# Two fused transformer blocks on one core: the instruction order derived with the other machine model

## The chip, the cores and the metric

The kernel runs on one core of a Trainium2 chip. Its engines are TensorE (PE, with its weight load shown apart as PEld), VectorE (DVE), ScalarE (ACT), GpSimd (POOL) and SyncE (SP, which here issues transfers). The metric is the device time in microseconds. Three runs of the kernel before took 1939.66, 1941.54 and 1941.79 us, median 1941.54 us.

## The reference

The input is one sequence of 512 tokens of width 1024, all in float32. It goes through two blocks of one layer each.

```
first_block:
  proj = rmsnorm(x) @ w_in            # 9792 columns: z, xbc, dt, q, k, v, gates
  y_ssd  = ssd_branch(...)            # conv + silu, 32 heads, two directions, chunks of 128 tokens
  y_attn = window_attention(q, k, v, ...) @ w_attn_out
  x = x + rmsnorm((g_ssd * y_ssd + g_attn * y_attn) @ w_o)
  x = x + rmsnorm(square(relu(rmsnorm(x) @ w_mlp_in)) @ w_mlp_out)
second_block:
  x = x + parallel_mixer(rmsnorm(x))  # mLSTM heads and latent causal attention, then one product
  x = x + memory_cross_attention(rmsnorm(x), rmsnorm(mem))
  x = x + square(relu(rmsnorm(x) @ w_ff1)) @ w_ff2
```

## The kernel before

**Products.** All large products use float32r, whose operands are split in two parts (`hi + lo`). Each product takes three matmuls per tile of 128 rows: hi by hi, lo by hi and hi by lo (lines 266 to 268 where channels are the output's partitions, `cm`; lines 284 to 286 where tokens are, `tm`). A full `cm` step is 24 matmuls of 512 columns into one PSUM bank `psg`, of which there are two; in the SSD stage it is cut into two half steps of 12. A `tm` step is 24 matmuls of 256 columns.

**Weights.** They come as a stream of units of 1 MB. SP loads a unit into one of two `raw` buffers (line 129), ACT casts it to `whi` in two halves (line 140) and DVE subtracts to get `wlo` (line 141). `use()` asks for the split of the next unit while the present one is multiplied.

**Stages.** First norm and the decays (about 0 to 50 us). The SSD branch in eight groups of four heads (to about 520 us, with a plain output product at 300 to 350 us). Window attention in eight pairs of heads with the gates between them (to 850 us). A residual norm (850 to 910), the first feed-forward (to 1240), the mixer and the attention to the memory (to 1600), the second feed-forward (to the end).

**What sets the order.** The body is traced as one straight list of instructions, the source order. In the SSD stage each group's steps and the next group's products (`f0` to `f7`) are listed by hand, and so are those of the mixer (`SEQ`) and of the attention to the memory (`XSEQ`):

```
GSEQ = """
z0 w0 xt1 st0 z1 w1 z2 z3 st1 silu st2 y0 f0 f1 y1 rows f2 f3 w2 e0 y2 e1 w3 f4 f5 bt cb y3 norm f6 e2 f7 u0 u1 xt0 e3
"""
```

The source order isn't the order that the engines get. When the `TileContext` is left, the framework plays the list through a model of the machine. In it an instruction can be issued when its inputs are ready in the model's time and its buffer is free, and where several can, the one that is earlier in the source goes first. The order in which the model issued them is then fixed for each engine. On the chip each engine runs its own list in that order and stops at an instruction whose semaphore has not come, with everything behind it. A few places bind the order by hand: `tc.issue_after` (lines 165, 182, 443, 559) and `tc.keep_in_program_order` (line 394).

**Lines that the prediction speaks of.** `late` and `dt_evac` with the round trip of the decays through DRAM (`csd`, `gld`, lines 500 and 513, fetched on POOL's queue at 626 and 628); the exponents (663 to 670); the convolution with its silu (567 to 573); `to_tokens` (578, 579); `cb` (634); `weights` (675); `y` (683 to 702); `norm` (707) and `u_channels` (712, which ends in `split_from`, 317 and 318).

Of the kernel before, what the change touches and what calls it, by code (L numbers as in the profile page):

```python
# [43 lines left out]
# columns of w_in  # L44
Z0, XBC0, DT0, Q0, K0, V0, G0 = 0, 2048, 6144, 6208, 7232, 7488, 7744
# columns of w_in_2
U0, VM0, OP0, IF0 = 0, 512, 1024, 1536

# columns of the packed constants
# [3 lines left out]
def packed_constants():  # L53
    """Constants that depend on shapes alone: the identity and its mirror image, the rotary
    frequencies, the one-hot of the relative position buckets, and the fixed rows of the products
    that make the exponents of the decays."""
# [11 lines left out]
    # rows 0..7 choose the chunk, rows 64..127 the pair that a token is in  # L68
# [4 lines left out]
    # rows 8..15 choose the head, rows 64..127 hide the pairs of tokens that a direction doesn't see  # L73
# [11 lines left out]
def body(ctx, tc, a, out, dbg=None):  # L85
# [26 lines left out]
    # ---------------------------------------------------------------- weights, as a stream of blocks  # L112
    win, win2 = a["w_in"][0], a["w_in_2"][0]

    class Unit:
        """A block of weights [128, kt, n], split into two parts of float32r whose sum it is."""
# [36 lines left out]
    def use(key, lag=False):  # L153
        """The unit; the next one is split at once or, with lag, where ahead() says."""
        stream[pos[key]].split()
        if not lag:
            ahead(key)
        return unit_of[key]

    def ahead(key, *behind):  # L160
        """The next unit being split, behind the given instructions, and the one after it on its way."""
        i = pos[key]
        with ExitStack() as order:
            for ins in behind:
                order.enter_context(tc.issue_after(ins.ins))
            for u in stream[i + 1 : i + 2]:
                u.split()
        for u in stream[i + 2 : i + 3]:
            u.load()

    def evac_first(key, evac, *args):
        """evac, with the next unit's split behind the first of it on each engine."""
# [78 lines left out]
    # ---------------------------------------------------------------- helpers  # L251
    def cm(key, act, evac, parts=1):
        """Steps of a channel-major product: evac(j, psum) for each 128 columns of the unit, each in
        one step or more."""
# [19 lines left out]
    def tm(key, act, evac, ntile=NT):  # L274
        """Steps of a token-major product: evac(t, psum) for each 128 tokens."""
# [20 lines left out]
    def weave(main, side):  # L296
        """The steps of both lists, each list spread evenly."""
# [13 lines left out]
    def split_from(src, hi, lo, gain=None):  # L311
        """hi + lo = src * gain (a column of gains), both float32r."""
# [7 lines left out]
    def inv_rms(dst, ssq, n, width):  # L320
        """dst = (ssq / n + eps) ** -0.5 for [128, width] columns."""
# [3 lines left out]
    def token_sums(ssq, tag="t"):  # L325
        """Sums over the partitions of [128, 512], token-major in PSUM [128, 4]."""
# [5 lines left out]
    def bcast_tokens(r, tag="t"):  # L332
        """[128, 4] token-major -> PSUM [128, 512] on every partition."""
# [5 lines left out]
    # ---------------------------------------------------------------- persistent tiles  # L339
# [17 lines left out]
    # ---------------------------------------------------------------- block 1, first norm  # L357
# [12 lines left out]
    # the tensor engine's clock is at its full rate when the first inputs are here  # L370
# [34 lines left out]
    # ---------------------------------------------------------------- parameters, as columns  # L405
# [34 lines left out]
    # ---------------------------------------------------------------- dt and the decays  # L440
# [14 lines left out]
    # what the products for the exponents take: see ssd_exponents  # L455
# [4 lines left out]
    def dt_evac(_, po):  # L460
        """Rows (half, direction, head), two chunks of tokens in each half."""
# [17 lines left out]
        # cumulative sums of dt * a in each chunk, forwards and backwards  # L479
# [13 lines left out]
        # cs in two float32r parts, by way of DRAM, where the heads of a group are one row  # L493
# [8 lines left out]
        # the logarithm of dt, less cs, in two parts too  # L502
# [11 lines left out]
        # token-major: exp(cs) and dt * exp(tot - cs)  # L514
# [14 lines left out]
        def late():  # L529
# [8 lines left out]
            # the decay over a whole chunk, on every partition; step k takes chunk k and chunk 3 - k  # L538
# [25 lines left out]
    # ---------------------------------------------------------------- block 1, SSD branch  # L564
# [22 lines left out]
    class Group:  # L587
        """The SSD branch of one group of four heads."""
# [5 lines left out]
        # products, convolution and layouts  # L594
# [27 lines left out]
        # rows of the products for the exponents  # L622
# [32 lines left out]
        def exponents(self, c):  # L655
            """dt[s] exp(cs[l] - cs[s]) of both directions: cs[l] comes from rows 0..7,
            log(dt) - cs[s] from rows 8..15; rows 64..127 hide what overflows on the wrong side, and
            the select what is next to the diagonal."""
# [110 lines left out]
    # ---------------------------------------------------------------- block 1, window attention  # L769
# [8 lines left out]
    # the bias over relative positions, one row for each head, read back as a Hankel block: the  # L778
    # queries of each block are taken in reverse
# [18 lines left out]
    def keys(kv):  # L798
        """The two parts of the keys of a head, each on both halves of the partitions."""
# [11 lines left out]
    def q_steps(u, parts=1):  # L811
        """Queries of a head, in reverse in each block: one part on its own half of the partitions,
        the other part on the other half."""
# [935 lines left out]
```

## Time and profile before

| what | value |
|---|---|
| three runs, median | 1941.54 us |
| profiled execution, first to last instruction (its span) | 1939.5 us |
| what the profile gives of its time outside the span | nothing; the three runs lie 0.2 to 2.3 us above the span |
| PE busy | 1868.0 us, 96% |
| weight load (PEld) busy | 1541.4 us, 79% |
| DVE, ACT, POOL busy | 1083.4 us (56%), 856.8 us (44%), 482.8 us (25%) |
| mean granted TensorE clock | 0.992 of full speed |

Read it from PE down: PE has a record open in 96% of the span, so 71.5 us of the span have none. A matmul's record is longer than the distance to the next one, so the distance between starts, not the length of a record, tells the rate. The other engines' shares say little by themselves: they are averages over stages, and in the SSD stage DVE is busy three quarters of the time, in the feed-forwards a third.

### The profile page before, as it was taken

The page shows a single profiled execution, that of the slowest core. Times are in us where ns is not written, and L with a number is a line of the kernel's source. Part 1 is how long each engine was busy: PE and PEld are TensorE (multiplying, and loading weights), DVE is VectorE, ACT ScalarE, POOL GpSimd, SP SyncE. Part 2 cuts the span into 40 slices and gives each one's busy share as a digit, 9 for nine tenths or more (in the row PEclk, how much of TensorE's full clock was granted, in tenths as well). Part 3 has the DMA queues.
Part 4 walks back from the last instruction along what each step waited for, and adds up shares of the span by engine and source line. Part 5 has one row for each costly group of instructions (what it writes and reads, how often), then busy time and mean ns, then how long its engine had stood idle before and what let it go on. Part 6 is the DMA issues. An engine that isn't in the chain of part 4 may idle for free. (4 is left out here: it accounts for less than half of the span.)

```text
span 1939.5 us, 24660 instructions
## 1 busy us (share of the span) xinstructions
PE 1868.0 (96%) x9685; PEld 1541.4 (79%) x9685; DVE 1083.4 (56%) x1751; ACT 856.8 (44%) x1397; POOL 482.8 (25%) x530
## 2 busy tenths in 40 slices
PE   8989999999999999998999999989999999999999
PEld 6878778887887777887888888888877778888887
DVE  7767773777555654537334334667567763334543
ACT  5655652755335665345332323444453543323231
POOL 1544450444202221233011202322110431111020
PEclk9999999999999999999999999999999999999999
DMA  6222122221222221333333332322111213232322
GB/s 174 68 67 67 45 67 87 67 67 44 82 94 82 82 78 66 119 122 109 98 109 98 101 94 89 114 73 74 51 45 65 87 44 108 90 107 87 109 87 65
DMA packets 169377, 164.10 MB, mean 85 GB/s; under 512 B 8742, under 2 KB 165101, under 8 KB 169262
## 3 DMA queue, kind: packets, MB, share of 16 engines
q1 hardware_dynamic: 157322, 151.03, 24.8%
q10 hardware_dynamic: 9444, 9.89, 1.6%
q0 software_dynamic: 2496, 1.61, 0.3%
q8 instruction: 76, 1.25, 0.3%
q14 instruction: 39, 0.32, 0.1%
HBM read 158.26 MB, written 4.23 MB: 84 GB/s over the span
## 5 line engine op out<-in xcount | busy, mean ns | idle before, releaser
L141 DVE TENSOR_TENSOR wlo<-raw,whi 128x1024 fp32r<-128x1024 f32 (+2 forms) x285 | 374.9, 1329 | 277.8 <-ACT whi L140 275.4
L140 ACT CAST whi<-raw 128x1024 fp32r<-128x1024 f32 (+2 forms) x285 | 288.3, 1029 | 408.9 <-PE psg L267 381.1
L266 PE MATMUL psg<-hh,whi 128*128 128x512 f32 (+1 forms) x1016 | 403.0, 397 | 0.8 <-DVE hl L318 0.8
L267 PE MATMUL psg<-hl,whi 128*128 128x512 f32 (+1 forms) x1016 | 400.7, 394 | 0.0
L268 PE MATMUL psg<-hh,wlo 128*128 128x512 f32 (+1 forms) x1016 | 399.3, 393 | 0.0
L266 PE MATMUL psg<-ua_h,whi 128*128 128x512 f32 x800 | 316.5, 396 | 0.5 <-DVE xT L1562 0.5
L267 PE MATMUL psg<-ua_l,whi 128*128 128x512 f32 x800 | 313.4, 392 | 0.0
L268 PE MATMUL psg<-ua_h,wlo 128*128 128x512 f32 x800 | 312.3, 390 | 0.0
L266 PEld LDWEIGHTS psg<-hh,whi 128*128 128x128 f32 (+1 forms) x1016 | 191.0, 188 | 40.5 <-issue 1.2
L268 PEld LDWEIGHTS psg<-hh,wlo 128*128 128x128 f32 (+1 forms) x1016 | 190.7, 188 | 39.7
L267 PEld LDWEIGHTS psg<-hl,whi 128*128 128x128 f32 (+1 forms) x1016 | 190.8, 188 | 38.1 <-DVE hl L315 0.4
L1164 POOL TENSOR_TENSOR fsq<-relu 128x512 f32<-128x512 f32 x64 | 80.9, 1264 | 507.9 <-ACT relu L1161 434.5
L266 PEld LDWEIGHTS psg<-ua_h,whi 128*128 128x128 f32 x800 | 150.1, 188 | 35.4 <-DVE xT L1562 2.4
L267 PEld LDWEIGHTS psg<-ua_l,whi 128*128 128x128 f32 x800 | 150.3, 188 | 32.3 <-DVE ua_l L1165 1.2
L268 PEld LDWEIGHTS psg<-ua_h,wlo 128*128 128x128 f32 x800 | 150.2, 188 | 30.7
L284 PE MATMUL psg<-whi,hh 128*128 128x256 f32 x416 | 121.5, 292 | 2.7 <-ACT sz L608 2.7
L286 PE MATMUL psg<-whi,hl 128*128 128x256 f32 x416 | 121.8, 293 | 0.0
L285 PE MATMUL psg<-wlo,hh 128*128 128x256 f32 x416 | 120.5, 290 | 1.0 <-DVE wlo L141 1.0
L986 POOL TENSOR_TENSOR ssq<-ssq,sq 128x512 f32<-128x512 f32 x42 | 66.4, 1582 | 117.0 <-ACT sq L985 116.0
L1165 DVE TENSOR_TENSOR ua_l<-fsq,ua_h 128x512 fp32r<-128x512 f32 x64 | 47.3, 739 | 79.2 <-POOL fsq L1164 79.2
L284 PEld LDWEIGHTS psg<-whi,hh 128*128 128x128 f32 x416 | 81.5, 196 | 5.9 <-ACT sz L608 4.0
L285 PEld LDWEIGHTS psg<-wlo,hh 128*128 128x128 f32 x416 | 81.4, 196 | 1.6 <-DVE wlo L141 1.2
(560 smaller groups left out, 2910.4 us busy)
## 6 DMA issues: line engine op xcount, KB each, us to landing
raw<-in_w_in_dram SPq DMA_DIRECT2D x37, 1024.0 KB
raw<-in_w_ff_dram SPq DMA_DIRECT2D x32, 1024.0 KB
raw<-in_w_mlp_in_dram SPq DMA_DIRECT2D x16, 1024.0 KB
raw<-in_w_mlp_out_dram SPq DMA_DIRECT2D x16, 1024.0 KB
raw<-in_w_in_dram SPq DMA_DIRECT2D x16, 512.0 KB
raw<-in_w_ssd_out_dram SPq DMA_DIRECT2D x8, 1024.0 KB
raw<-in_w_attn_out_dram SPq DMA_DIRECT2D x4, 1024.0 KB
raw<-in_w_o_dram SPq DMA_DIRECT2D x4, 1024.0 KB
```

Source lines behind the costliest of these rows:

```text
L140: A.copy(self.hi[sl], self.raw[sl])
L141: V.tensor_tensor(out=self.lo[sl], in0=self.raw[sl], in1=self.hi[sl].bitcast(F32), op=ALU.subtract)
L266: T.matmul(o, lhsT=u.hi[:, k, c:e], rhs=xh[k], start=k == 0, stop=False)
L267: T.matmul(o, lhsT=u.hi[:, k, c:e], rhs=xl[k], start=False, stop=False)
L268: T.matmul(o, lhsT=u.lo[:, k, c:e], rhs=xh[k], start=False, stop=k == u.kt - 1)
L284: T.matmul(o, lhsT=xh[k][:, tk], rhs=u.hi[:, k, 0 : u.n], start=k == 0, stop=False)
L285: T.matmul(o, lhsT=xh[k][:, tk], rhs=u.lo[:, k, 0 : u.n], start=False, stop=False)
L286: T.matmul(o, lhsT=xl[k][:, tk], rhs=u.hi[:, k, 0 : u.n], start=False, stop=k == u.kt - 1)
L986: G.tensor_tensor(out=self.t, in0=self.t, in1=q, op=ALU.add)
L1164: G.tensor_tensor(out=f, in0=r, in1=r, op=ALU.mult)
L1165: V.tensor_tensor(out=ua_l[:, m, :], in0=f, in1=ua_h[:, m, :].bitcast(F32), op=ALU.subtract)
```

## The change

One argument is added where the kernel opens the framework's context. The machine model that the scheduler plays the source order through is another one, which follows each engine's queue of issued instructions and the semaphores between the engines, and has its own durations. The source order, the instructions, the buffers and the hand-made bindings stay. The rest of the diff replaces comments and docstrings by blank lines, so that line numbers stay too.

```diff
-    with tile.TileContext(nc) as tc:
+    with tile.TileContext(nc, schedule_with_timeline_sim=True) as tc:
         body(tc, aps, out)
```

## Rows read from the trace of the kernel before

**Rows 1.** The page: each engine's busy time, share of the span and instructions
```profile
PE 1868.0 (96%) x9685; PEld 1541.4 (79%) x9685; DVE 1083.4 (56%) x1751; ACT 856.8 (44%) x1397; POOL 482.8 (25%) x530
```

**Rows 2.** Busy time by stage: length, PE, PEld, DVE, ACT, POOL, clock, DMA share, GB/s
```profile
0.00:40.00 40.00, 37.57 (x194) 30.44 (x195) 28.96 (x66) 22.80 (x39) 6.21 (x21) 1.00 0.60 174
40.00:300.00 260.00, 234.06 (x1330) 199.81 (x1329) 196.52 (x286) 150.79 (x231) 121.49 (x173) 0.96 0.23 67
350.00:520.00 170.00, 159.13 (x915) 134.44 (x914) 126.83 (x191) 95.93 (x149) 69.62 (x97) 0.99 0.20 61
520.00:850.00 330.00, 328.57 (x1796) 265.02 (x1796) 168.11 (x358) 162.00 (x305) 73.11 (x53) 1.00 0.30 96
850.00:910.00 60.00, 54.95 (x289) 44.21 (x288) 41.09 (x48) 31.22 (x51) 22.66 (x15) 1.00 0.24 72
910.00:1240.00 330.00, 330.00 (x1472) 273.10 (x1471) 125.99 (x137) 105.92 (x142) 52.12 (x44) 1.00 0.32 102
1240.00:1600.00 360.00, 338.91 (x1977) 276.09 (x1976) 248.05 (x510) 169.21 (x321) 89.08 (x89) 1.00 0.21 66
1890.00:1939.50 49.50, 44.81 (x212) 36.57 (x210) 17.97 (x25) 8.29 (x13) 0.22 (x1) 0.98 0.21 64
```

**Rows 3.** PE's waits, whole span: waiting line, releaser, us in total, times, longest
```profile
PE psc L634 <- ACT cT L573: 8.6, 6, 2.3
PE pse L663 <- DMA lh<-gld: 6.9, 1, 6.9
PE pst L712 <- DVE ua_l L318: 5.8, 4, 2.6
...
PE pst L712 <- DVE sz L707: 4.7, 5, 1.3
PE pst L578 <- DVE ua_l L318: 4.7, 4, 1.6
```

**Rows 4.** PE in order of time, SSD: start, length, line, tiles, count [idle before]
```profile
215.63 0.39 PE L266 MATMUL psg<-hh,whi 128*128 128x512 f32 x1
...
218.12 0.39 PE L268 MATMUL psg<-hh,wlo 128*128 128x512 f32 x1
218.35 0.94 PE L712 MATMUL pst<-ident,sz 128*128 128x128 f32 x4
...
227.71 0.28 PE L285 MATMUL psg<-wlo,hh 128*128 128x256 f32 x1
229.57 0.66 PE L578 MATMUL pst<-ident,cacc 128*128 128x128 f32 x4 [1.58 <-DVE ua_l L318]
229.99 0.36 PE L286 MATMUL psg<-whi,hl 128*128 128x256 f32 x1
```

**Rows 5.** All engines in order of time: the first exponents, columns as in rows 4
```profile
49.99 1.19 PE L663 MATMUL pse<-rh,lh 128*128 128x512 f32 x2 [6.93 <-DMA lh<-gld]
```

**Rows 6.** One of six stretches with a lowered granted clock, columns as in rows 2
```profile
44.00:56.00 12.00, 6.01 (x35) 5.76 (x36) 9.49 (x15) 6.01 (x9) 1.41 (x6) 0.72 0.64 184
```

**Rows 7.** ACT by line: count, busy us, mean ns, idle before and releasers
```profile
L140 ACT CAST whi<-raw 128x1024 fp32r<-128x1024 f32 (+2 forms) x285 | 288.3, 1029 | 408.9 <-PE psg L267 381.1 <-issue 11.4 <-PE pse L1226 9.6
L1162 ACT ACTIVATE ua_h<-relu 128x512 fp32r<-128x512 f32 x64 | 40.4, 631 | 0.9
...
L665 ACT ACT_TABLE_LOAD x25 | 32.1, 1283 | 0.4
L573 ACT ACT_TABLE_LOAD x23 | 29.5, 1283 | 0.4
```

**Rows 8.** ACT in order of time: a table load between two functions, columns as in rows 4
```profile
55.05 1.28 ACT L665 ACT_TABLE_LOAD   x1
56.35 0.60 ACT L665 ACTIVATE e<-pse 128x512 f32<-128x512 f32 x1
```

**Rows 9.** DVE by line, columns as in rows 7
```profile
L141 DVE TENSOR_TENSOR wlo<-raw,whi 128x1024 fp32r<-128x1024 f32 (+2 forms) x285 | 374.9, 1329 | 277.8 <-ACT whi L140 275.4 <-PE psc L1296 2.2
```

**Rows 10.** The load queue's own longest wait, columns as in rows 3
```profile
SPq L129 <- DVE wlo L141: 1463.4, 121, 39.2
```

## The prediction

> **What bounds the kernel now.** I read the stage table first, then PE's waits, then PE in order of time in one SSD group. PE is the bound: a record is open for 1868.0 of 1939.5 us [rows 1]. The reader is to see in the stage table that the 71.5 us without one lie in few places [rows 2]. In the feed-forward (910 to 1240) PE is open for 330.00 of 330 us. The idle time of the others, as length less PE: start 2.4, SSD to 300 us 25.9, SSD from 350 us 10.9, attention 1.4, the residual norm 5.1, mixer and memory 21.1, the end 4.7. The sum is 71.5. So the order can change about 58 us of idle time, 36.8 in the SSD stage and 21.1 in the mixer, and it can add more.
>
> What ends the waits is a chain through other engines: silu to the products of the group (8.6 us), a fetched row of decays (6.9), evacuated PSUM banks (5.8 and 4.7) [rows 3]. DVE is busy for 196.5 of 260 us in the SSD stage, ACT for 150.8 [rows 2], so a chain step there finds another one in front of it most of the time.
>
> The clock has a part of its own. From 40 to 300 us the mean granted clock is 0.96 [rows 2], because PE runs at 1.2 instead of 2.4 GHz in stretches that follow idle time, such as 0.72 over 12 us with PE open for half of them [rows 6]. The deficit is 0.04 x 260 + 0.01 x 170 = 12.1 us of full rate, and PE has work in nine tenths of it: 10.9 us. Over 36.8 us of idle time that is 0.3 us lost again for each idle us. I multiply added or removed idle time in this stage by 1.3.
>
> **The change, part by part.** It removes and adds no arithmetic and no transfer. It moves instructions within each engine's list. Since every engine stops at its first instruction that isn't ready, a move costs when it puts a step that isn't ready in front of work that is, or puts the chain's step behind work that could have waited. Both are in the trace. At 227.71 us four transposes (L578) stand inside a run of products and hold it for 1.58 us although the next matmul of it (L286) is ready [rows 4]. The other way round, four transposes (L712) come behind a half step of 12 matmuls from 215.63 to 218.12 us: 2.49 us for 11 distances, 0.226 each, so 2.72 us for a half step [rows 4].
>
> *Feed-forwards, 910 to 1240 and 1600 to 1890: nothing.* A step of 24 matmuls lasts 24 x 0.226 = 5.4 us. Beside it ACT has an evacuation, a square (0.63 each by the square's row) and half of a unit's cast (1.03): 2.3 us [rows 7]; DVE has a split (1.33) and one more operation [rows 9]. With the two accumulator banks, an evacuation placed behind both casts is 2.1 us late and still early. If that cover were gone it would cost the 2.1 us once for each step; I take 0, bounds 0 and +2. The load queue waits 1463 us in all for buffers that `wlo` frees, on average 12 us [rows 10], so it has nothing to be reordered for; a split that comes later by one step moves the load behind it by as much, and PE has a whole unit of 10.9 us before it needs that.
>
> *Start: -2 us, bounds -7 and +5.* PE stands for 6.93 us at the first exponents [rows 5], which wait for the decays' way through DRAM. The transfer's time stays. A model with other transfer times may put ready work before them: at most the whole 6.93 us is filled. If the chain on DVE falls behind one unit's split (two of 1.33) and on ACT behind its cast (two of 1.03), it is 4.7 us longer. It is nearer to the first, since the stall shows that the old model took the rows as landed; but the ready work in the source is small, so a third.
>
> *SSD groups: +12.4 us, bounds -20 and +25.* What is to move is the interleaving of the next group's products with this group's chain. In a model that follows queues, matmuls that are ready are taken into PE's queue, and a transpose that gets ready a little later finds them in front. The unit of that delay is the half step, 2.72 us. Nothing is lost while PE works off such a step; it is lost at the group's end, where the chain then ends later and the products are used up. There are seven transitions between groups, and each already has PE waiting for the chain (nine waits at L712 alone if the second releaser of 4.7 us is counted in), so slack there is nil. Bounds: a full half step each, 7 x 2.72 x 1.3 = 24.8; or the waits at L712 and L578 (5.8 + 4.7 + 4.7) all go, -15.2 x 1.3 = -19.8. I take half a half step, 7 x 1.36 x 1.3 = 12.4, as those nine waits last 1.2 us on average.
>
> *Attention 520 to 850: 0, bounds -1.4 and +5.* PE is open for 328.6 of 330 us; ACT and DVE are busy half of the time [rows 2] and cover a moved step; the upper bound is two half steps. *Residual norm: 0, bounds -1 and +3*: one chain, whose order its data give.
>
> *Mixer and memory: +7 us, bounds -12 and +21.* 21.1 us of idle time in 360 [rows 2], DVE at 69%. The source order is a long hand-made list of short steps of four heads, as sensitive as the SSD list; I take the same share of its idle time, 12.4 / 36.8 = a third. Lower bound: over half of it goes; upper: it doubles.
>
> *Table loads: 0 in the forecast.* The order on ACT decides how often exponential and silu alternate. Now 25 loads stand before exponentials and 23 before silus, 1.283 us each, with 0.4 us of idle time before each of the two groups in all [rows 7]. They are followed without a gap too: a load begins at 55.05 and its exponential at 56.35 [rows 8], so a switch takes 1.30 us.
>
> The Trainium skill (ScalarE: Activation LUTs, section What ACT_TABLE_LOAD costs) counts a drain of about 1.38 us on top, 2.66 us for each switch. This trace doesn't agree: 1.30 us from start to start. By the page every switch that the new order adds would cost twice as much as in the rival on table loads below.
>
> Sum: -2 + 12.4 + 7 = +17.4 us on the span of 1939.5 us, 1956.9. The median of the runs lies 2.0 us above the span, so I predict 1959 us.
>
> **The rivals.**
>
> *The other order fits the chip better (faster).* One mechanism: steps that the old model held for ready too early, and that now stop PE in front of ready work, are put later. For it: the 1.58 us hold at 229.57 [rows 4], the 6.93 us at 49.99 [rows 5], and clock stretches that follow such holds. Against it: most of the waits end with a busy DVE, which another order does not make faster. Price: 4 us of the first wait and a third of the 15.2 us at L712 and L578, 9 x 1.3 = 12; in the mixer 3 of 21.1. That gives 1939.5 - 15 + 2 = 1927 us, from 1914 to 1937. It decides when the removed holds outweigh the delayed chains, which cost 1.36 us for each transition.
>
> *Nothing that counts moves (same).* The two accumulator banks, the two weight buffers and the data dependences leave each engine little choice, so that only steps with slack change places. For it: the feed-forwards, where no wait is left. Against it: in rows 4 steps of both kinds are within one another, so the list there hangs on readiness to a fraction of a us. Time: 1938 to 1945 us.
>
> *ACT's order falls apart (much slower).* The SSD stage has 40 silus and 32 pairs of exponentials. If each silu got its own load, and each exponential run between them, there would be 80 loads in place of the 48 now: 32 x 1.283 = 41 us on ACT, whose share in the stage goes from 57% (150.8 + 95.9 of 430 us [rows 2]) to 67%. The largest of PE's waits that ends with ACT is 8.6 of 71.5 us [rows 3], an eighth, so 41 / 8 x 1.3 = 7 us come through. With a mixer at its upper bound, 14 above what I took, this is 1941.5 + 17.4 + 7 + 14 = 1980 us. Against it: nothing in the change is about tables.
>
> **How the numbers follow.** Forecast (slower by 4 to 35 us) 0.44; better fit 0.31; same 0.13; much slower 0.12. A difference under 0.2%, 3.9 us, can't be told from none. So faster 0.31, within 0.2% 0.13, slower 0.56. The forecast's own range is 1946 to 1976 us (its upper end all half steps at full price). The range of 1920 to 1992 us leaves out the lower third of the better fit and the upper half of the worst case, together 0.16; it is wide because both signs have weight.
>
> **What would show it.** The stage table of the new profile: idle time between 40 and 520 us up from 36.8 to about 46 us, in the mixer from 21 to 28, none in the feed-forwards. PE's waits: more at L712, L578 and L634, less at L663. The lists: the same counts but for table loads. Granted clock in the SSD stage below 0.96. I am wrong if idle time in the SSD stage falls, if a feed-forward shows waits (then the evacuations' order was not covered), or if the time went into a stage where I put 0.

## The result, and the profile after

The changed kernel takes 2022.6 us (median of four runs, 2021.4 to 2024.2), the kernel before in the same session 1941.5 us: 1.0419 times as long, 95% interval [1.0404, 1.0434], or 81 us more. The direction is the one forecast, the size is almost five times the forecast's 17.4 us, and the time lies beyond the upper end of the range.

The page's line of the engines, to be read against [rows 1]:

```profile
PE 1906.0 (94%) x9685; PEld 1581.4 (78%) x9685; DVE 1068.5 (53%) x1751; ACT 842.1 (42%) x1384; POOL 480.6 (24%) x530
```

The counts are the same but for 13 fewer on ACT. The span has grown from 1939.5 to 2019.7 us; PE's time without a record from 71.5 to 113.7 us (2019.7 less 1906.0), and the time with one by 38.0 us, for the same matmuls. Where this happened is told by marks that every trace has, such as the last transpose of the SSD stage (L712). Twelve matmuls, some 2.7 us by their distance of 0.226 us, stand behind the first of these marks before and ahead of it after; the other sections hold the same number of matmuls.

| section, by PE's instructions | before | after | more |
|---|---|---|---|
| start to the last L712 (start and SSD stage) | 512.2 us | 578.8 us | +66.6 |
| to the first L1022 (attention, gates, residual norm) | 367.5 | 375.1 | +7.6 |
| to the first L1224 (memory and first feed-forward) | 372.5 | 368.3 | -4.2 |
| to the last L1022 (mixer, attention to the memory) | 349.8 | 360.2 | +10.4 |
| to the end (second feed-forward) | 337.5 | 337.4 | -0.1 |

Inside the first row, the last L712 of each of the eight groups gives the period of a group:

| | end of the first group | from each group's end to the next |
|---|---|---|
| before | 116.4 us | 54.0, 54.1, 54.4, 93.4, 54.0, 54.6, 31.3 |
| after | 128.8 | 62.9, 64.1, 64.4, 92.8, 63.4, 60.4, 42.0 |

The first group is 12.4 us late, and every later one adds 6 to 11 us, save the one with the plain output product in it (93.4 and 92.8), where there is other work for PE. The seven periods have grown by 54.2 us together. Of these, 32.0 us are time in which PE has no record open (24.8 us before, 56.7 after, from the first group's end to the last L712), and 22.2 us are records open for longer.

One stage of the changed kernel and one stretch at the end of a group, columns as in [rows 2] (the fixed cut falls on somewhat other work, since the groups are later):

```profile
40.00:300.00 260.00, 222.15 (x1183) 189.86 (x1182) 181.21 (x262) 137.69 (x207) 103.35 (x153) 0.87 0.19 57
...
178.00:198.00 20.00, 11.82 (x42) 9.22 (x43) 8.88 (x15) 6.99 (x14) 7.01 (x11) 0.50 0.01 2
```

From 40 to 300 us PE has work for 222.15 us at a mean clock of 0.87, before for 234.06 at 0.96 [rows 2]. The last line shows what the loss looks like at a group's end: no engine is busy for more than 59% of the time, hardly a transfer runs (0.01), and PE's granted clock is 0.50 (1.2 GHz). The mixer's section of the table, from mark to mark, in the kernel before and then in the changed one:

```profile
1252.20:1602.00 349.80, 329.51 (x1892) 266.54 (x1891) 241.02 (x502) 164.92 (x314) 87.29 (x87) 1.00 0.20 65
```

```profile
1322.20:1682.40 360.20, 341.65 (x1890) 280.06 (x1891) 239.75 (x500) 161.65 (x309) 82.74 (x82) 0.94 0.19 59
```

Here PE's time without a record did not grow (20.3 and 18.6 us); its records are open for longer, at a lower clock. PE's waits of the changed kernel, columns as in [rows 3]:

```profile
PE pse L663 <- ACT e L665: 24.5, 13, 2.9
PE psy L683 <- DVE xd L698: 16.4, 10, 3.9
PE pst L712 <- DVE sz L707: 10.2, 7, 5.0
PE pst L712 <- DVE ua_l L318: 9.4, 6, 1.6
PE psg L284 <- ACT sz L608: 6.6, 7, 1.0
```

They are the steps of one chain, from the exponentials through `y` and the norm to `u`. The wait for the fetched row `lh` and L634's for the silu, the two longest of [rows 3], are gone from the top.

PE in order of time, first the changed kernel where the second group's states are made (columns as in [rows 4]; the left-out lines are products of the same group's fill):

```profile
143.97 1.02 PE L645 MATMUL pso<-xw,bt 128*128 128x256 f32 x4
144.64 0.58 PE L266 MATMUL psg<-hh,whi 128*128 128x512 f32 x1
...
149.41 0.59 PE L645 MATMUL psy<-xw,bt 128*128 128x256 f32 x2
...
154.83 0.59 PE L645 MATMUL pso<-xw,bt 128*128 128x256 f32 x2
...
155.71 0.33 PE L683 MATMUL psy<-xt,w 128*128 128x64 f32 x2
```

and the same steps of the same group in the kernel before:

```profile
123.85 1.45 PE L645 MATMUL pso<-xw,bt 128*128 128x256 f32 x4 [0.17 <-DVE xw L642]
...
129.57 1.02 PE L645 MATMUL psy<-xw,bt 128*128 128x256 f32 x4
...
131.46 0.80 PE L683 MATMUL psy<-xt,w 128*128 128x64 f32 x6
```

Before, the first state and `y0` of this group lie 7.6 us apart; after, 11.7 us. In the fourth group it is 4.1 and 11.5 us. After, PE works off some 20 matmuls of the fill, nearly a full step of 24, between the first state and the second, and some 20 again between the second and the third; `y0` follows two matmuls behind the third. Before, products stand only between the first and the second. The fill is what the source lists behind `y0`, so less of it is left when the end of the chain needs something beside it. Whether the period hangs on this is tried below (the fill behind `y0`). That end, in the changed kernel:

```profile
180.35 1.97 PE L683 MATMUL psy<-xt,w 128*128 128x64 f32 x8 [3.87 <-DVE xd L698]
183.52 1.28 PE L663 MATMUL pse<-rh,lh 128*128 128x512 f32 x2 [1.20 <-ACT e L665]
186.67 1.28 PE L663 MATMUL pse<-rh,lh 128*128 128x512 f32 x2 [1.87 <-ACT e L665]
...
191.00 1.12 PE L712 MATMUL pst<-ident,sz 128*128 128x128 f32 x4 [1.56 <-DVE ua_l L318]
193.16 0.58 PE L284 MATMUL psg<-whi,hh 128*128 128x256 f32 x1 [1.04 <-ACT sz L608]
```

Even the next group's z (L284) can't help: 48 of its 96 matmuls have been done ahead already, both accumulators hold them, and their evacuation waits until `u` has read the one buffer `sz`.

### The profile page after: what moved, and what is told of

Its sections match the earlier page's. It is cut to its first block, busy times and chain, and to the rows that moved or that the text cites. A ratio compares the mean times of both kernels' runs of the same rounds, so it can differ in the third digit from the quotient of the medians.

```text
span 2019.7 us, 24623 instructions
## 1 busy us (share of the span) xinstructions
PE 1906.0 (94%) x9685; PEld 1581.4 (78%) x9685; DVE 1068.5 (53%) x1751; ACT 842.1 (42%) x1384; POOL 480.6 (24%) x530
## 4 chain that ended last, share of the span: by engine, by line
PE 82%; DVE 8%; ACT 4%; POOL 3%; issue 2%; DMA 1%; SPq 0%; ACTq 0%; DVEq 0%; POOLq 0%
PE psg L266 20%; PE psg L267 20%; PE psg L268 20%; PE psg L284 2%; PE psg L285 2%; PE psg L286 2%; DVE wlo L141 1%; PE pse L858 1%; POOL w L670 1%; DVE cacc L572 1%; POOL xd L697 1%; PE pst L712 1%; ACT whi L140 1%; PE pse L1470 1%; PE pso L906 1%
## 5 line engine op out<-in xcount | busy, mean ns | idle before, releaser
L141 DVE TENSOR_TENSOR wlo<-raw,whi 128x1024 fp32r<-128x1024 f32 (+2 forms) x285 | 348.0, 1253 | 268.0 <-ACT whi L140 267.3
L140 ACT CAST whi<-raw 128x1024 fp32r<-128x1024 f32 (+2 forms) x285 | 279.9, 1030 | 408.2 <-PE psg L267 385.6
L1164 POOL TENSOR_TENSOR fsq<-relu 128x512 f32<-128x512 f32 x64 | 86.8, 1357 | 499.6 <-ACT relu L1161 463.6
L284 PE MATMUL psg<-whi,hh 128*128 128x256 f32 x416 | 128.0, 308 | 9.2 <-ACT sz L608 6.6
L285 PE MATMUL psg<-wlo,hh 128*128 128x256 f32 x416 | 125.4, 302 | 1.3 <-DVE wlo L141 1.3
L284 PEld LDWEIGHTS psg<-whi,hh 128*128 128x128 f32 x416 | 86.6, 208 | 13.7 <-ACT sz L608 9.3
L285 PEld LDWEIGHTS psg<-wlo,hh 128*128 128x128 f32 x416 | 86.4, 208 | 3.5 <-DVE wlo L141 1.5
```

Of the source, the lines that this page charges most:

```text
L140: A.copy(self.hi[sl], self.raw[sl])
L141: V.tensor_tensor(out=self.lo[sl], in0=self.raw[sl], in1=self.hi[sl].bitcast(F32), op=ALU.subtract)
L284: T.matmul(o, lhsT=xh[k][:, tk], rhs=u.hi[:, k, 0 : u.n], start=k == 0, stop=False)
L285: T.matmul(o, lhsT=xh[k][:, tk], rhs=u.lo[:, k, 0 : u.n], start=False, stop=False)
L1164: G.tensor_tensor(out=f, in0=r, in1=r, op=ALU.mult)
```

## The experiments

**Exchanged orders.** Each of these kernels is traced once with one model, to read the order in which it issues every engine's instructions, and then built with the other model with chosen engines held to the order that was read, by edges that order without a wait. The stage SSD goes from the first group's rows to the last group's `u`. Their lines stand 3 further down (L715 is L712 of the listing).

```diff
...
+        for k in order:
+            ins = traced[k]
+            if k not in keep or str(ins.engine).split(".")[-1] != e:
+                continue
+            if last is not None:
+                tc.add_manual_dep(ins, last.name, mybir.DependencyInfo(mybir.DependencyClass.NoSync, mybir.DependencyReason.DATA),
+                                  reason="pin")
+            last = ins
...
-    with tile.TileContext(nc, schedule_with_timeline_sim=True) as tc:
+    with tile.TileContext(nc, schedule_with_timeline_sim=model, name="kernel") as tc:
         body(tc, aps, out)
+        pin(tc, traced, order, engines, stage)
```

*TensorE alone* (`ENGINES, STAGE = ('PE',), 'ssd'`).

> The changed kernel, but TensorE alone takes its instructions of the SSD stage in the order that the kernel before has there; VectorE, ScalarE, GpSimd and SyncE keep the order of the changed model, inside the stage and outside it. The last L712 stands at 512.2 us before and 578.8 us after, so 66.6 of the 80.2 us of span were lost up to there. Theory 1 (TensorE takes the fills and the next group's z ahead of the chain state, y, E, u, each chain step queues behind whole product steps, and the products are used up when the group ends): nearly all of the 66.6 us come back, last L712 at 512 to 530 us, time 1955 to 1975 us. Rival (the orders of VectorE, ScalarE and GpSimd, with splits and convolutions ahead of what the chain needs, carry the loss): less than 20 us come back, time above 2002 us.

*The others without TensorE* (`('DVE', 'Activation', 'Pool')`).

> The changed kernel, but VectorE, ScalarE and GpSimd take their instructions of the SSD stage in the order that the kernel before has there; TensorE keeps the changed order. Theory 1 (TensorE's order carries the 66.6 us): the last L712 stays at 565 to 585 us and the time at 2010 to 2030 us, or worse, since two orders that were not made together can cross. Rival (the orders of the other engines carry it): last L712 below 535 us, time below 1980 us.

*All engines.*

> The changed kernel, but all engines take the SSD stage in the order of the kernel before; what lies behind the stage keeps the changed order. If the stages add up, the last L712 is at 512 to 516 us and the time is 2022.6 - 66.6 = 1956 us (1950 to 1962), the 13.6 us left being the section with the window attention (+7.6), the mixer (+10.4) and the memory (-4.2). If the later stages lost because the SSD stage handed them work in another state, less is left: 1941 to 1949 us.

*TensorE and ScalarE.*

> The changed kernel; TensorE and ScalarE take the SSD stage in the order of the kernel before, the other engines keep the changed one. So far: TensorE alone gave back 18 us (2004.4), VectorE, ScalarE and GpSimd together nothing (2024.3), all engines 58.7 us (1963.9). Theory 1, now with a partner (TensorE's order alone leaves u waiting for sz: 18.6 us in 9 waits, since ScalarE takes the exps of the next group ahead of the Square that the norm waits for, and VectorE two weight splits ahead of the norm): ScalarE's order gives back a part, 10 to 25 us beyond TensorE's, time 1980 to 1995 us. Rival (VectorE is the partner): within 6 us of 2004.

*TensorE and VectorE.*

> The same with TensorE and VectorE. If VectorE is the partner that keeps TensorE's order from paying (the norm's four scalings behind two weight splits of 1.2 us each, xd behind the convolution), the period of a group falls from 60 to 54 to 56 us and the time to 1970 to 1985 us. If ScalarE is the partner, the time stays at 1995 to 2006 us. Either way the first group's end stays late (134.4 us by the first run, 116.4 before) as long as the rows lh come late.

*TensorE, VectorE, ScalarE.*

> The changed kernel; TensorE, VectorE and ScalarE take the SSD stage in the order of the kernel before, GpSimd and SyncE in the changed one. TensorE and VectorE gave 1980.6 us, all engines 1963.9: 16.7 us are left, 9.1 of them at the end of the first group (134.1 against 125.0 us). If ScalarE holds them (it takes exps and weight casts ahead of the copies that TensorE's transposes and products feed), the time is 1964 to 1968 us. If GpSimd does (the fetches of lh and rh stand in its queue behind work that waits), it stays within 4 us of 1980.

*TensorE, VectorE, GpSimd.*

> The changed kernel; TensorE, VectorE and GpSimd take the SSD stage in the order of the kernel before. With TensorE and VectorE the last L712 stands at 536.7 us, with ScalarE as well at 532.4, with all engines at 520.6. If GpSimd is the third engine that the chain needs (the adds of xd, the masks of the exponentials and the fetched rows are all its own), the last L712 comes at 520 to 526 us and the time at 1964 to 1970 us. If it needs ScalarE and GpSimd together, it stays at 530 us or later, time 1974 to 1982 us.

*The opposite exchange.*

> The opposite exchange: the kernel before (old model), all its engines taking the SSD stage in the changed order. If the order inside the stage is the cause, the last L712 comes at 565 to 580 us instead of 512 and the time is 1941.5 + 58 (what all engines gave back the other way) = 1995 to 2008 us. If the loss came from the state in which the earlier stage hands over (weights, DMA), the time stays below 1965 us.

Measured (ratios to the kernel before, run on the same chip in the same session; the orders behind the stage are derived anew in each kernel, so the marks inside the stage are the better measure of it). The first group's end hangs on what lies ahead of the stage as well, so the last two columns leave it out. The marks come from one profiled execution of each kernel:

| SSD stage in the order of before | time, us | ratio, 95% interval | last L712, us | given back of 66.6 | first group's end to the last L712, us | given back of 54.2 |
|---|---|---|---|---|---|---|
| no engine (changed kernel) | 2022.6 | 1.0419 [1.0404, 1.0434] | 578.8 | | 450.0 | |
| VectorE, ScalarE, GpSimd | 2024.3 | 1.0433 [1.0416, 1.0450] | 579.6 | -0.8 | 444.6 | 5.4 |
| TensorE | 2004.4 | 1.0327 [1.0311, 1.0342] | 557.3 | 21.5 | 422.9 | 27.1 |
| TensorE, ScalarE | 2011.5 | 1.0357 [1.0340, 1.0374] | 568.8 | 10.0 | 439.6 | 10.4 |
| TensorE, VectorE | 1980.6 | 1.0200 [1.0185, 1.0215] | 536.7 | 42.1 | 402.6 | 47.4 |
| TensorE, VectorE, ScalarE | 1980.5 | 1.0197 [1.0183, 1.0211] | 532.4 | 46.4 | 402.4 | 47.6 |
| TensorE, VectorE, GpSimd | 1976.6 | 1.0161 [1.0136, 1.0186] | 527.4 | 51.4 | 395.1 | 54.9 |
| all five | 1963.9 | 1.0117 [1.0101, 1.0132] | 520.6 | 58.2 | 395.6 | 54.4 |
| kernel before, SSD stage in the changed order | 2014.1 | 1.0370 [1.0355, 1.0386] | 582.9 | (512.2 before) | 450.9 | (395.8 before) |

Both single-engine theories fall. With TensorE's changed order nearly the whole loss is there, with the other orders changed (the first row) or with those of three engines put back (the second), so its order suffices for the loss, as theory 1 said; orders that were not made together may cost something of their own, which these kernels can't tell apart. But its old order alone gives back half of what the periods lost, not nearly all. The old orders of TensorE and VectorE together give back 47.4 of the 54.2 us, and with GpSimd's the whole, while ScalarE adds nothing with VectorE and takes some back without it. VectorE and GpSimd weren't tried without TensorE each by itself.

Not every range was met. TensorE alone lies in the rival's by its time. TensorE with ScalarE is slower than either of its cases. All five lie 2 us above the time and 5 us above the last L712 that were expected. TensorE with VectorE and GpSimd stands between its two cases by the last L712, and by its time in the second. The opposite exchange goes beyond the upper end. The direction of this one is clear even so: it loses 70.7 us by the last L712 and 55.1 in the seven periods. So the order inside the stage is the cause, in either model's surroundings.

All five restore the old periods to 0.2 us (54.0, 53.9, 54.4, 93.4, 54.0, 54.6, 31.3) and leave 8.4 us, from the first group. There TensorE stands for 13.7 us at the first exponents (6.9 before), for the fetched row of decays, whose way begins ahead of the stage.

How VectorE's order does it is seen in the kernel with TensorE's old order, where u waits for the norm:

```profile
PE pst L715 <- DVE sz L710: 18.6, 9, 3.2
```

VectorE of that kernel in order of time, from the last chunk's `sz` to the norm (L710):

```profile
242.57 0.42 DVE L702 TENSOR_TENSOR sz<-xd,sz 128x256 f32<-128x256 f32 x1
245.31 0.22 DVE L325 TENSOR_SCALAR ssg<-ssg 128x4 f32<-128x4 f32 x1 [2.32 <-ACT xd L705]
245.54 0.69 DVE L678 TENSOR_TENSOR w<-psc,w 128x512 f32<-128x512 f32 x1
246.25 1.23 DVE L144 TENSOR_TENSOR wlo<-raw,whi 128x1024 fp32r<-128x1024 f32 x1
247.39 1.14 DVE L710 TENSOR_SCALAR sz<-sz,ssg 128x256 f32<-128x256 f32 x4
```

and of the kernel before, where these lines are L699, L322 and L707:

```profile
214.32 0.42 DVE L699 TENSOR_TENSOR sz<-xd,sz 128x256 f32<-128x256 f32 x1
...
215.37 0.17 DVE L322 TENSOR_SCALAR ssg<-ssg 128x4 f32<-128x4 f32 x1
...
216.71 0.35 DVE L707 TENSOR_SCALAR sz<-sz,ssg 128x256 f32<-128x256 f32 x1
```

From `sz` to the norm it is 2.39 us before and 4.82 us here: VectorE first stands for ScalarE's square, then takes a weight split ahead of the norm.

**The order behind the stage.**

> The changed kernel, but behind the SSD stage (attention, residual norm, memory, mixer, second feed-forward) all engines take the order of the kernel before; the SSD stage keeps the changed order. If the 13.6 us that are lost there (7.6 in the section of the attention, 10.4 in the mixer, less the 4.2 of the memory) belong to that order: 2009 us (2006 to 2012). If they are handed over by the late SSD stage: 2018 us or more.

Measured: 2012.7 us, 1.0360 [1.0344, 1.0375], just above the first theory's range. The mixer's section takes 348.3 us (360.2 changed, 349.8 before), the attention's 371.0 (375.1), and the memory's goes back to 372.6. So the mixer's loss is its own order's. The attention's is not settled: with the old order it still takes 3.5 us more than before, behind a changed SSD stage, but in the kernel of all five, where the SSD stage is the old one and the rest changed, it takes 375.9, no less than in the changed kernel. How much of it goes with the SSD stage stays open.

**Single edges in the changed model.** Two kernels bind TensorE, one VectorE.

```diff
+            def fills(i=i):
+                with tc.issue_after(q.done[0].ins):
+                    run(fill[len(fill) * i // NF : len(fill) * (i + 1) // NF])
+            todo[f"f{i}"] = fills
-            todo[f"f{i}"] = lambda i=i: run(fill[len(fill) * i // NF : len(fill) * (i + 1) // NF])
```

*The fill behind y0.*

> The changed model with one edge more in each group: no product step of the fill (f0 to f7) may be issued on TensorE ahead of the last matmul of the group's y0, where the source order has them too. Theory 1 in its narrow form (the fills taken early delay the four states and y0 by three product steps and are missing between y1, y2 and y3): the period of a group falls from about 65 us to about 56, the last L712 to 515 to 540 us, the time to 1960 to 1985 us, and the granted clock of 40:300 rises from 0.87 to 0.95 or more. If the next group's z, which stay early, hold both accumulators while they wait for sz, less than half comes back: 1990 to 2015 us. Rival (the other engines' orders): nothing comes back, above 2010 us.

Measured: 2014.4 us, 1.0375 [1.0360, 1.0391]; last L712 at 571.9. The time lies in the second case's range: 8.2 us come back, of the seven periods' growth 3.4 us. Most periods stay at 60 to 62 us, one falls to 55.6, and the one with the output product grows from 92.8 to 104.3. The edge did what it was to do; at the beginning of the second group PE now stands:

```profile
138.83 0.80 PE L663 MATMUL pse<-rh,lh 128*128 128x512 f32 x1 [3.36 <-ACT e L665]
...
143.11 0.80 PE L663 MATMUL pse<-rh,lh 128*128 128x512 f32 x1 [3.48 <-ACT e L665]
144.09 2.07 PE L645 MATMUL pso<-xw,bt 128*128 128x256 f32 x4 [0.18 <-DVE xw L642]
...
148.68 1.10 PE L683 MATMUL psy<-xt,w 128*128 128x64 f32 x8
```

The second group's period, cut at PE's first instruction of each step, in us; in brackets the part of it with a PE record open:

| from, to | before | changed | fill behind `y0` |
|---|---|---|---|
| last u of the first group to the first state | 7.5 (5.8) | 15.2 (14.2) | 18.8 (10.7) |
| first state to `y0` | 7.6 (7.5) | 11.7 (11.7) | 4.6 (4.5) |
| `y0` to y3 | 7.2 (7.2) | 12.0 (12.0) | 9.7 (8.9) |
| y3 to the first u | 24.2 (23.4) | 20.0 (13.2) | 24.3 (24.2) |
| first u to the last | 7.5 (4.9) | 3.9 (2.2) | 4.9 (4.8) |

The states are no longer late among themselves, and PE has work from y3 to the last u. Yet what it stood there it now stands at the group's beginning, for the exponentials, and the period is 62.2 us instead of 62.9. So the fill ahead of the states isn't by itself what the period hangs on.

*The next group's z behind u as well* (`order.enter_context(tc.issue_after(gs[g - 1].turned0.ins))` around each z).

> The changed model with two edges in each group: the fill's product steps behind the last matmul of y0 (that alone gave 8 us: 2014.4), and the next group's four z behind the first block of u of the group before. If the z, taken early, hold the accumulators while sz is in use, and that is the rest of what TensorE's order does, the time is that of TensorE's order alone or a little better: 1995 to 2008 us. If the two edges leave free what the model then hoists in their place (E, T, states), nothing more comes back or it gets worse: 2010 to 2030 us.

Measured: 2006.4 us, 1.0330 [1.0315, 1.0346]; last L712 at 563.6, so by the time two edges give nearly what TensorE's whole old order gives (2004.4). Of the seven periods' growth they give back 13.0 us, TensorE's whole old order 27.1. What is late next is in this kernel's waits:

```profile
PE pso L645 <- DVE xw L642: 28.8, 9, 4.8
```

ScalarE of the same kernel in order of time, ahead of the copy of `xt` that `xw` reads:

```profile
255.06 1.99 ACT L140 CAST whi<-raw 128x1024 fp32r<-128x1024 f32 x2
257.07 1.28 ACT L620 ACT_TABLE_LOAD   x1
258.37 1.06 ACT L620 ACTIVATE sz<-sz 128x1024 f32<-128x1024 f32 x1
259.33 0.57 ACT L579 COPY xt<-pst 128x512 f32<-128x512 f32 x1
```

Two casts, a table load and a silu stand ahead of a copy on which the states hang. The wait that now tops the list stands at the group's beginning.

*The decays' chain first* (`with tc.issue_after(dt_done[0].ins):` around VectorE's part of each convolution).

> The changed model with one edge: VectorE's instructions of every convolution behind the last step of the decays' chain (the subtract at L510). In the changed kernel VectorE mixes 20 of them and six weight splits into that chain: the first scan (L487) starts at 51.40 us, at 34.42 before, and the first exponents at 67.8, at 50.0 before. If this mixture is what delays the first group by 12.4 us, the first exponents start at 50 to 56 us, the first group ends at 116 to 120 us instead of 128.8, and the time falls by 8 to 13 us, to 2010 to 2015. If the first group is bound by TensorE's and ScalarE's order like the later ones, the rows come early and the group still ends at 126 to 130 us: time 2019 to 2024 us.

Measured: 2030.0 us, 1.0452 [1.0438, 1.0466], slower than the changed kernel. The first exponents do come early; the row of L663 in the changed kernel and of the same line, L664, in this one (least, median and longest in ns, first and last start in us):

```profile
L663 PE MATMUL pse<-rh,lh x64: 389/480/988, 67.8 to 521.1; 128*128 128x512 f32 x64
```

```profile
L664 PE MATMUL pse<-rh,lh x64: 389/477/796, 54.6 to 528.6; 128*128 128x512 f32 x64
```

Yet the first group ends at 135.7 us instead of 128.8. Both of the expectation's cases fall: an early row alone doesn't help. The convolutions, pushed back, bring `cb` later (first L634 at 73.9 us, 47.7 in the changed kernel), which may be what costs here. What holds the first group in the changed kernel isn't separated further.

**The clock.** Both kernels keep the changed order on every engine and add matmuls at the end of a group, into a bank that u0 overwrites. The lines of both stand further down: in the first, L287 is L284 of the listing and L724 is L712; in the second, L674 is L663, L698 is L683 and L715 is L698. The cut is the second one's:

```diff
+    def hold(pt, n, anchor=None):
...
+            for _ in range(n):
+                ins = T.matmul(pt, lhsT=h_act[0][0][:, 0:P], rhs=h_act[0][0], start=True, stop=True).ins
...
+                hold(self.pt0, COUNTS[0])
             for h in range(4):
```

*Thirty-six of them, ahead of y3, u0 and u1.*

> The changed kernel with its order on every engine, and in six of the seven transitions between groups 36 matmuls of 128x512 that nothing reads, put on TensorE where it waits at the group's end: 16 ahead of y3, 14 ahead of u0, 6 ahead of u1 (0.226 us each at full rate, some 8 us of TensorE's time for a group). In the changed kernel 134 of the 539 us of the stage are at the lowered clock, 82 of these with TensorE busy, so that at most 82 - 19 = 63 us more than before run at half rate. Theory 3 (the half rate itself carries a good share): with the waits filled the low stretches shrink to below 70 us, and the last L712 comes 15 to 32 us earlier, time 1991 to 2008 us. If the chain through VectorE and ScalarE sets the period whatever the clock: the low stretches shrink too, but the last L712 stays within 8 us of 578.8, or comes later by what the added matmuls delay the chain, time 2016 to 2035 us.

*Sixteen, only around y3.*

> The changed kernel with its order on every engine, and in six of the seven transitions 16 matmuls of 128x512 that nothing reads, only where TensorE waits: 10 ahead of y3 (2.3 us at full rate, the wait there is 2.6 to 3.9 us) and 6 behind it (1.4 us, the wait for the exponents behind it is 1.2 to 2.2 us). They can't delay the chain by more than a few tenths. Theory 3 (the half rate itself carries a good share of the 66.6 us): at the end of a group y3 lasts 1.97 us at half rate instead of 1.00, and the exponents, u and the first z run at half rate as well, some 3 to 6 us for a group, so that with fewer low stretches the last L712 comes 15 to 32 us earlier, time 1991 to 2008 us. If the waits for ScalarE and VectorE set the period and the half rate mostly falls into them: low stretches fall from 134 to below 90 us, the last L712 moves by less than 8 us, time 2015 to 2026 us.

Measured: 2043.3 us, 1.0514 [1.0498, 1.0529], with the last L712 at 598.7 us, above both ranges; and 2025.4 us, 1.0425 [1.0408, 1.0443], with the last L712 at 583.2, in the range of the second case. The stretches at the lower level in the SSD stage, added up from the trace's clock records, are 134 us in the changed kernel, 67 in the first of the two and 104 in the second, which was to be below 90. The second kernel around y3:

```profile
180.19 2.43 PE L593 MATMUL pst<-hh 128*128 128x512 f32 x10
184.25 1.10 PE L698 MATMUL psy<-xt,w 128*128 128x64 f32 x8 [1.62 <-DVE xd L715]
185.16 2.06 PE L593 MATMUL pst<-hh 128*128 128x512 f32 x6
187.42 1.28 PE L674 MATMUL pse<-rh,lh 128*128 128x512 f32 x2 [0.20 <-ACT e L676]
```

y3 takes 1.10 us instead of 1.97, and the exponents still start 3.17 us behind y3, as in the changed kernel: what the clock gives falls into the wait for the exponentials. From the first group's end to the seventh's it is 409.0 us, 408.0 in the changed kernel. So the half rate cost nothing in this wait. Behind the waits it does cost, as the first kernel shows: its u0 comes late, because the 14 matmuls stood behind the last exponents at half rate (5.71 us):

```profile
192.55 5.71 PE L593 MATMUL pst<-hh 128*128 128x512 f32 x14
198.10 0.60 PE L724 MATMUL pst<-ident,sz 128*128 128x128 f32 x4
...
203.41 0.39 PE L287 MATMUL psg<-whi,hh 128*128 128x256 f32 x1 [1.04 <-ACT sz L616]
203.63 0.28 PE L288 MATMUL psg<-wlo,hh 128*128 128x256 f32 x1
203.75 0.27 PE L289 MATMUL psg<-whi,hl 128*128 128x256 f32 x1
```

The same y3 is 4.8 us later than in the changed kernel and z 10.2 us later, so these matmuls delay the chain by 5.5 us; the next group's first state is only 7.8 us later (214.9 against 207.1). The z that run at full rate, 0.12 us apart instead of 0.21, have given 2.5 us back. Six such transitions are an estimate of 15 us for the clock, of 66.6, worked out from one transition; no run shows it. The upper bound for the seven periods is the 22.2 us by which PE's records are open for longer.

By the test of the second expectation theory 3, by which 15 to 32 us were to come back, falls: nothing did. Two kernels above point the same way. From the first group's end to the last L712 the changed kernel has 112 us at the lower level. With the old orders of VectorE, ScalarE and GpSimd it is 56 us, with the fill behind `y0` 69, and they give back 5.4 and 3.4 of the 54.2 us. The waits come first.

**What to do with it.** Two kernels with the old model:

*The changed order for the memory alone* (the pin over the section from the residual norm to the end of the first feed-forward).

> The kernel before, but all engines take the section of the memory (the residual norm, the memory's keys and the first feed-forward) in the changed order. From the first L1022 to the first L1224 the changed kernel is the faster one, 368.3 against 372.5 us with the same 1665 matmuls in between, since the products of the memory stand under the norm's chain. If that order alone does it, the time is 1941.5 - 4.2 = 1937.3 us (1935 to 1939), faster than both kernels. If the 4.2 us are paid in the attention before it (375.1 against 367.5 us), where those products were taken from, it is 1941 to 1945 us.

*The first exponents behind z1* (`with tc.issue_after(held):`, `held` being the last matmul of z1).

> The kernel before with one edge: the first group's exponents behind its z1 on TensorE, as the changed order has them, so that TensorE does not stand 6.9 us for the row lh. If the wait only has to be filled: 1935 to 1939 us. If the exps on ScalarE, which then come some 8 us later, set the end of the first group: 1940 to 1946 us.

Measured: 1939.6 us, 0.9982 [0.9974, 0.9991], and 1941.4 us, 0.9994 [0.9982, 1.0006]. The first is the fastest of all, by 3.2 us of its own session's 1942.8, a gain of 0.2% whose interval leaves out 1, somewhat less than the 4.2 expected; the section itself falls from 372.5 to 366.8 us and the attention's before it rises by 1.9. In the second the SSD stage ends 1.4 us earlier, and no difference in time can be told.

## Why the prediction was right or wrong

The step that failed is the term of the SSD groups: "the unit of that delay is the half step", of which I took half for each of seven transitions, times 1.3, +12.4 us, with a full half step (+24.8) as the bound. In place of it the seven periods grew by 54.2 us together, 8.9 to 10.7 us in five of them, where I had 1.8. Three things in that step were wrong.

- *One step late instead of a whole chain.* I priced one chain step that finds a half step in front of it, where [rows 4] shows it in the old order. In the trace the second and the third state each found some 20 matmuls in front of it, and `y0` stands behind both. But this delay isn't the price either: the edge that takes it away gives back 3.4 us of the 54.2.
- *What was late next.* I wrote that the loss comes at the end, where "the products are used up", and gave it no price of its own. The trace has that end: 20 us with PE open for 11.82. The edge that takes the fill away from the states gave the end its fill back, and PE stood at the group's beginning instead. How the loss divides among the steps of the chain stays open.
- *One engine instead of several.* I read the order as PE's. By the exchanges PE's changed order suffices for nearly the whole loss, but its old order gives back only 27.1 us, with VectorE's 47.4, and with GpSimd's all. [rows 2] pointed at why: DVE busy for 196.5 of 260 us, so that its order decides as well when a chain step comes.

The multiplier 1.3 for the clock was too small as a ratio: in the seven periods 22.2 us of longer records beside 32.0 us of more idle time, a factor of 1.7. Not all of the open time need be lost time; how much of it is isn't shown.

*Start, -2 (bounds -7 and +5):* wrong. The wait at L663 for the row was filled, as I thought, but the row came 17.8 us later (67.8 against 49.99 [rows 5]): VectorE mixes convolutions and weight splits into the decays' chain, where I had allowed for one split of it. The first group ended 12.4 us later. With the whole old order of the stage 8.6 us of that remain, where TensorE waits for the row; in the changed order an early row alone doesn't help.

*Attention, 0 (bounds -1.4 and +5):* wrong by 7.6 us, of which the old order behind the stage takes back 4.1. *Mixer and memory, +7 (bounds -12 and +21):* the section takes 10.4 us more, within the bounds, but that is luck: I had its idle time rising by a third, from 21 to 28 us, and from mark to mark it fell from 20.3 to 18.6, while PE's records were open for 12.1 us longer at a clock of 0.94 instead of 1.00. *Residual norm, 0 (bounds -1 and +3), and first feed-forward, 0:* the section that holds the memory's keys and both of them is 4.2 us shorter, since the norm's chain now has products of the memory under it; the old model with this order gains 3.2 us in all. *Second feed-forward, 0:* right; it takes 337.4 against 337.5 us.

*Table loads:* the rival falls. There are fewer loads on ACT, 69 for 82, and fewer of the two kinds in [rows 7], 21 and 17 for 25 and 23:

```profile
L665 ACT ACT_TABLE_LOAD x21 | 26.9, 1283 | 0.4
L573 ACT ACT_TABLE_LOAD x17 | 21.8, 1283 | 0.3
```

*What would show it:* the SSD stage's idle time rose from 36.8 us to 74.1 (40 us to the last L712), not to 46, and its granted clock fell below 0.96, as written, to 0.87. More waits came at L712, as written. But those at L578 and L634, which I had growing, left the head of the list, and those at L663, which I had falling, lead it, now for the exponentials instead of the row. The wait at L683, the second, I hadn't named. The range failed with its bound: a full half step for each transition was taken for the worst the order could do in this stage, and it wasn't.

## What to carry to other kernels

An order that takes ready work first puts the fill of a loop ahead of the chain's early steps and leaves less of it for the late ones. Both are seen in this trace, but neither is a price: undoing the first gave back 3.4 of 54.2 us, because the chain waited elsewhere. So look for what waits next before a delay is multiplied by the number of groups. Where several engines share a chain, exchange their orders in groups as well as singly, and leave out what came late ahead of the loop: here TensorE's old order alone gave back half of what the periods lost, those of the three other engines a tenth, TensorE's with VectorE's nearly nine tenths, and with GpSimd's all.

## What the runs showed of the hardware

VectorE's step of the convolution with two operands in SBUF (L572) lasts 0.75 us at the median and up to 2.2 us, here in the changed kernel (one of its two groups):

```profile
L572 DVE SCALAR_TENSOR_TENSOR cacc<-cbuf,pv,cacc x64: 734/752/2208, 45.9 to 524.9; 128x512 f32<-128x512 f32 x64
```

Sixteen of all 128 last longer than 1.2 us, and each of them overlaps with work of GpSimd, but so do 26 of the 90 that last no longer than 0.8 us. VectorE and then GpSimd of the changed kernel in order of time:

```profile
175.82 4.13 DVE L572 SCALAR_TENSOR_TENSOR cacc<-cbuf,pv,cacc 128x512 f32<-128x512 f32 x2
```

```profile
176.16 0.75 POOL L697 TENSOR_TENSOR xd<-xd,yo 128x256 f32<-128x256 f32 x1
...
177.42 0.76 POOL L694 TENSOR_TENSOR xd<-xt,dskip 128x256 f32<-128x256 f32 x1
178.15 1.25 POOL L670 TENSOR_TENSOR w<-e,e 128x512 f32<-128x512 f32 x1
```

The Trainium skill (SBUF — State Buffer, section SBUF: two separate sides) says that the two engines share a pair of ports as an exclusive lock, which a VectorE instruction with two SBUF inputs and a GpSimd instruction that reads SBUF take in turns. The long ones are compatible with it; the trace doesn't show which of the overlapping operations read SBUF at the same time, and no run here tried it. The total didn't grow with the change: what all L572 last beyond 0.745 us adds up to 19.6 us before and 19.9 us after.
